# Doubling eight triangular inverses in one chain, with half of them held in the other head's partitions

## The chip, the cores and the metric

The kernel runs on one core of a Trainium2 chip. The metric is the device time of one execution in microseconds. Before the change it is 2000.85 us, the median of 3 runs (1999.77 to 2000.95).

## The reference, cut to what matters

Two transformer blocks run one after the other on 512 tokens of width 1024. The second block has a mixer with two groups of 8 heads: stick-breaking attention, and the RWKV-7 recurrence that is touched here. For each head and each token, with a 64 x 64 state S,

```
S_t = S_{t-1} diag(w_t) + (S_{t-1} a_t) b_t^T + v_t k_t^T ;  y_t = S_t r_t
```

The kernel computes it in 8 chunks of 64 tokens. Inside a chunk the vectors S_{t-1} a_t depend on one another through a strictly triangular 64 x 64 matrix A, so the inverse of a unit triangular matrix, (I - A)^-1, is wanted for each chunk and head: 8 chunks x 8 heads. Everything is in fp32.

## The kernel before

The second block's mixer is `mix2`. Heads are taken two at a time, four times (f = 0 to 3): head one lies in partitions 0 to 63, head two in 64 to 127. For each f, `rw_solve` prepares the chunk matrices and their inverses, and `rw_scan` (of the f before, at the same time) carries the state over the 8 chunks. After them come the stick-breaking heads.

All small products are 64 x 64 x 64 in fp32. `pair` (L400) issues one product for each of the two heads, with rows and output in the same half of the partitions: two opposite corners of the 128 x 128 array. `turn` is a `pair` with the identity, which transposes. In the trace each fp32 product is two MATMUL instructions with a load of weights each, so a pair is four.

The inverse is found by doubling, in `double(q)` (L1905 to L1934), for q = 0 (chunks 0 to 3) and q = 1 (chunks 4 to 7) as two chains of steps that run beside each other. A tile `tmt` holds for four chunks the inverse so far (index 1) and its transpose (index 0). First the transposes are made (4 turns, a ScalarE copy at L1913). Then there are five levels (blocks of 2, 4, 8, 16, 32):

- step one: 4 pairs, A times the transpose, into a PSUM bank, and VectorE masks the level's blocks out of it into z (L1921);
- step two: 4 pairs for the transpose (`tmt`, z; not at the last level) and 4 pairs for the inverse (z, `tmt`) into the two halves of one bank, and VectorE adds both onto `tmt` (L1930; at the last level only the inverse, L1933).

Everything has a tag of PSUM banks: `c` has 3 banks in turn, used by the solve and by the norms and transposes of the stick-breaking queries, keys and values; `pt` has 3, used by the scan.

The order of TensorE's instructions is written at build time by `weave` (L409). It keeps a clock of its own, on which a pair costs 55 ns and half of its two products' time (`pair`, last line), a VectorE or ScalarE operation a fixed part and a part by its size (`after`, with `SEM` and `SEM2` for the way there and back). A stream (`rw_solve`, `rw_scan`, norms) that has to wait yields the time at which it can go on. While no stream is ready, `weave` puts in "fillers": matmuls 128 x 128 x 512 of the projections that the mixer has to make anyway (`sb_steps`, `rw_steps`, through `dense_steps`). It puts in as many as the wait needs at 214 ns each, at least four (`MINF`):

```
self.fill(max(MINF, math.ceil((t - self.clock) / 214)))
```

It also paces them, by `WORK[f]` and the supply of the period. The supply of a period is limited: a queue entry opens only when its period has come and when `heads` and `scans` have got far enough, and where none is open the clock jumps, and the engine really waits. In the trace all matmuls of these helpers have line L339.

Of the kernel before, what the change touches and what calls it, by code (L numbers as in the profile page):

```python
# [9 lines left out]
F32 = mybir.dt.float32  # L10
# [3 lines left out]
AF = mybir.ActivationFunctionType  # L14
OP = mybir.AluOpType
# [278 lines left out]
class K:  # L294
# [106 lines left out]
    def pair(self, o, l, r, start=False, stop=False):  # L401

        t = self.clock
        for hh in (0, 1):
            p = slice(64 * hh, 64 * hh + 64)
            self.mm(o(p), l(p), r(p), start=start, stop=stop)
        self.clock = t + 55 + (self.clock - t) / 2

    def turn(self, o, x):  # L409

        self.pair(o, x, lambda p: self.ident[p, p], True, True)
# [1385 lines left out]
    def rw_solve(self, f, u, ag):  # L1797

        nc, V, S, P, C = self.nc, self.nc.vector, self.nc.scalar, self.nc.gpsimd, self.C2
        yield lambda: (f, 1) in u  # L1800
        xk = u[f, 1]
        t2 = self.rt
# [8 lines left out]
        x = self.after("S", 512, self.after("V", 512))  # L1811
        t, kf, bo = self.tmp("rt"), xk, self.tmp("bo", "rt")
# [4 lines left out]
        for half in (0, 1):  # L1817
            ps = self.bank("c")
            for b2 in (0, 1):
                b = 2 * half + b2  # L1820
# [3 lines left out]
            w = lambda x: x[:, hs].rearrange("p (b t) -> p b t", b=2)  # L1824
# [15 lines left out]
        def tok(n, src):  # L1840
            ps = self.bank("c")
            for c in range(8):
                cs = slice(64 * c, 64 * c + 64)
                self.turn(lambda p: ps[p, cs], lambda p: src[p, cs])
            d = t2(f"tok{n}")
            S.activation(d, ps, AF.Copy)
            self.after("S", 512)
            return d

        yield lambda: (f, 0) in u  # L1850
        r = u[f, 0]
# [6 lines left out]
        vt = tok(2, v)  # L1858
        ar = self.rp.tile([128, 8, 2, 64], F32, name="ar", tag="ar", bufs=2)
# [10 lines left out]
        x = self.after("V", 1024)  # L1870
# [17 lines left out]
        x = self.after("V", 512)  # L1888
# [3 lines left out]
        yield from mat(0, bb)  # L1892
        ab, ak = mats

        bc = lambda x: x.unsqueeze(1).to_broadcast([128, 4, 64])
        tt = []
        for q in (0, 1):
            d = self.rp.tile([128, 2, 4, 64], F32, name=f"tmt{q}", tag=f"tmt{q}", bufs=2)
            V.tensor_tensor(d[:, 1], ab[:, 4 * q:4 * q + 4, 0:64], bc(C["m1t"]), op=OP.mult)
            V.tensor_tensor(d[:, 1], d[:, 1], bc(C["eye"]), op=OP.add)  # L1900
            x = self.after("V", 512)
            tt.append(d)
        self.rws = dict(ar=ar, ab=ab, ak=ak, bt=bt, kt=kt, vt=vt, tt=tt, dec=dec, bon=bon)

        sq4 = lambda ps: ps[:, 0:256].rearrange("p (c t) -> p c t", t=64)  # L1905

        def double(q):

            d = tt[q]
            ps = sq4(self.bank("c"))  # L1910
            for c in range(4):
                self.turn(lambda p: ps[p, c], lambda p: d[p, 1, c])
            S.activation(d[:, 0], ps, AF.Copy)  # L1913
            w = self.after("S", 256)
            for l in range(5):
                yield w
                ps = sq4(self.bank("c"))
                for c in range(4):
                    self.pair(lambda p: ps[p, c], lambda p: ab[p, 4 * q + c, 0:64], lambda p: d[p, 0, c], True, True)
                z = sq4(t2(f"z{q}", 256, 1))  # L1920
                V.tensor_tensor(z, ps, bc(C["lev"][:, 64 * l:64 * l + 64]), op=OP.mult)  # L1921
                yield self.after("V", 256)
                ps = self.bank("c").rearrange("p (i c t) -> p i c t", i=2, t=64)
                if l < 4:
                    for c in range(4):
                        self.pair(lambda p: ps[p, 0, c], lambda p: d[p, 1, c], lambda p: z[p, c], True, True)
                for c in range(4):
                    self.pair(lambda p: ps[p, 1, c], lambda p: z[p, c], lambda p: d[p, 1, c], True, True)
                if l < 4:
                    V.tensor_tensor(d, ps, d, op=OP.add)  # L1930
                    w = self.after("V", 512)
                else:
                    V.tensor_tensor(d[:, 1], ps[:, 1], d[:, 1], op=OP.add)  # L1933
                    w = self.after("V", 256)  # L1934

        yield x
        yield double(0), double(1)

    def rw_scan(self, f, u, o, g2, sg, w):

        nc, V, S, P, C = self.nc, self.nc.vector, self.nc.scalar, self.nc.gpsimd, self.C2
        ar, ab, ak, bt, kt, vt, tt, dec, bon = (w[k] for k in ("ar", "ab", "ak", "bt", "kt", "vt", "tt", "dec", "bon"))
        t2 = self.rt
        st = std = None
        y = o
        for c in range(8):
            cs = slice(64 * c, 64 * c + 64)
            tc = tt[c // 4][:, 1, c % 4]
            b = self.bank("pt")[:, 0:64]
            self.pair(lambda p: b[p], lambda p: ak[p, c, 0:64], lambda p: vt[p, cs], True, st is None)  # L1950
            if st is not None:
                yield w
                self.pair(lambda p: b[p], lambda p: ar[p, c, 0], lambda p: st[p], False, True)
            x = t2("xc", 64)
            S.activation(x, b, AF.Copy)
            w = self.after("S", 64)
            if st is not None and c < 7:
                std = t2("std", 64)
                V.tensor_scalar(std, st, dec[:, c:c + 1], None, op0=OP.mult)
                self.after("V", 64)  # L1960
            yield w
            b1 = self.bank("pt")[:, 0:64]
            self.pair(lambda p: b1[p], lambda p: tc[p], lambda p: x[p], True, True)
            u = t2("uc", 64)
            S.activation(u, b1, AF.Copy)
            w = self.after("S", 64)
            if c < 7:
                b2 = self.bank("pt")[:, 0:64]
                self.pair(lambda p: b2[p], lambda p: kt[p, cs], lambda p: vt[p, cs], True, False)
            yield w  # L1970
            if c < 7:
                self.pair(lambda p: b2[p], lambda p: bt[p, cs], lambda p: u[p], False, True)
                ns = t2("st", 64)
                if st is None:
                    V.tensor_scalar(ns, b2, dec[:, c:c + 1], None, op0=OP.mult)
                else:
                    V.scalar_tensor_tensor(ns, b2, dec[:, c:c + 1], std, op0=OP.mult, op1=OP.add)
                w = self.after("V", 64)
            b3 = self.bank("pt")[:, 0:64]
            self.pair(lambda p: b3[p], lambda p: vt[p, cs], lambda p: ak[p, c, 64:128], True, False)  # L1980
            self.pair(lambda p: b3[p], lambda p: u[p], lambda p: ab[p, c, 64:128], False, st is None)
            if st is not None:
                self.pair(lambda p: b3[p], lambda p: st[p], lambda p: ar[p, c, 1], False, True)
            V.tensor_copy(y[:, cs], b3)
            x = self.after("V", 64)
            if c < 7:
                st = ns

        yield x
        m = self.bank("pt")  # L1990
        self.mm(m, self.blk, y, start=True, stop=True)
        V.scalar_tensor_tensor(y, m, -1.0 / 64, y, op0=OP.mult, op1=OP.add)
        yield lambda: not self.squares
        self.squares = 1
        sq = t2("hsq", 512, 1)
        S.activation(sq, y, AF.Square)
        x = self.after("S", 512, self.after("V", 512))
        ps = self.bank("pt")
        self.mm(ps, g2[:, 128 * f:128 * f + 128], sg, start=True, stop=True)
        V.scalar_tensor_tensor(bon, bon, self.vec("rw_ln_b_2", f), ps, op0=OP.add, op1=OP.mult)  # L2000
        V.scalar_tensor_tensor(y, y, self.vec("rw_ln_w_2", f), ps, op0=OP.mult, op1=OP.mult)
        self.after("V", 1024)
        yield x
        rr = yield from self.root("pt", sq, 1.0 / 64, self.eps[1])
        self.squares = 0
        V.tensor_tensor(y, y, rr, op=OP.mult)
        self.roots -= 1
        yield self.after("V", 512)
        V.tensor_tensor(o, y, bon, op=OP.add)
        yield self.after("V", 512)  # L2010
        self.scans = f + 1
# [40 lines left out]
```

## Time and profile before

| what | value |
|---|---|
| median of 3 runs | 2000.85 us |
| the profiled execution's own time | 2004.94 us |
| its span, first to last instruction | 2003.1 us |
| TensorE matmuls, busy share of the span | 96% |
| TensorE weight loads, busy share | 74% |
| VectorE, ScalarE busy share | 54%, 39% |
| mean granted TensorE clock | 0.978 |
| mixer of the second block, solves and scans | about 1185 to 1515 us of the span |

Times are counted from the span's start. "Busy" is the time in which an instruction of the engine is under way; matmuls overlap one another, so their pace is read from the starts of successive groups in the timeline, not from their durations.

### The profile page before, as it was taken

The page shows a single profiled execution, that of the slowest core. Times are in us where ns is not written, and L with a number is a line of the kernel's source. Part 1 is how long each engine was busy: PE and PEld are TensorE (multiplying, and loading weights), DVE is VectorE, ACT ScalarE, POOL GpSimd, SP SyncE. Part 2 cuts the span into 40 slices and gives each one's busy share as a digit, 9 for nine tenths or more (in the row PEclk, how much of TensorE's full clock was granted, in tenths as well). Part 3 has the DMA queues.
Part 4 walks back from the last instruction along what each step waited for, and adds up shares of the span by engine and source line. Part 5 has one row for each costly group of instructions (what it writes and reads, how often), then busy time and mean ns, then how long its engine had stood idle before and what let it go on. Part 6 is the DMA issues. An engine that isn't in the chain of part 4 may idle for free.

```text
span 2003.1 us, 27567 instructions
## 1 busy us (share of the span) xinstructions
PE 1926.2 (96%) x11492; PEld 1475.2 (74%) x11492; DVE 1079.5 (54%) x1798; ACT 782.2 (39%) x1353; POOL 147.8 (7%) x117
## 2 busy tenths in 40 slices
PE   5889999889999998999999999999999999999999
PEld 2766666668888886888888877677667778888887
DVE  6588875662434346543434555565657674444343
ACT  3666776442323233322222453322335652222221
POOL 3340110130000002000000000000002200000000
PEclk8999999889999998999999999999999899999999
DMA  7124123312322221223232321110101022323222
GB/s 292 56 98 143 65 87 135 106 63 84 105 84 100 90 94 61 98 84 105 85 105 85 105 92 44 43 44 23 38 18 33 1 105 84 106 85 105 87 98 90
DMA packets 27342, 171.54 MB, mean 86 GB/s; under 512 B 3153, under 2 KB 3409, under 8 KB 9041
## 3 DMA queue, kind: packets, MB, share of 16 engines
q1 hardware_dynamic: 23472, 163.44, 23.4%
q10 hardware_dynamic: 3744, 6.34, 0.9%
q8 instruction: 90, 1.47, 0.3%
q14 instruction: 36, 0.29, 0.0%
HBM read 167.67 MB, written 2.10 MB: 85 GB/s over the span
## 4 chain that ended last, share of the span: by engine, by line
PE 80%; ACT 2%; DVE 2%; POOL 1%; issue 1%; DMA 0%; ACTq 0%; POOLq 0%; DVEq 0%
PE ps_mm L339 45%; PE ps_s L339 22%; PE ps_c L339 7%; PE ps_pt L339 4%; PE ps_o L339 1%; POOL xr L1308 0%; PE ps_pt L878 0%; ACT whi L243 0%; POOL x L1357 0%; DMA x<-in_x 0%; DVE wlo L249 0%; PE ps_mm L734 0%; DVE hl L1372 0%; DVE y L1356 0%; POOL hl L1315 0%
## 5 line engine op out<-in xcount | busy, mean ns | idle before, releaser
L243 ACT ACTIVATE whi<-w 128x1024 fp32r<-128x1024 f32 (+4 forms) x277 | 274.7, 994 | 787.0 <-PE ps_mm L339 481.5
L339 PE MATMUL ps_mm<-hh,whi 128*128 128x512 f32 x1304 | 528.7, 406 | 21.7 <-ACT whi L243 9.3
L339 PE MATMUL ps_mm<-hh,wlo 128*128 128x512 f32 x1304 | 528.7, 406 | 6.1 <-DVE wlo L249 6.1
L339 PE MATMUL ps_mm<-hl,whi 128*128 128x512 f32 x1304 | 529.6, 406 | 2.9 <-DVE hl L1315 1.2
L249 DVE TENSOR_TENSOR wlo<-w,whi 128x1024 fp32r<-128x1024 f32 (+7 forms) x316 | 325.2, 1036 | 155.8 <-ACT whi L243 155.4
L339 PEld LDWEIGHTS ps_mm<-hh,whi 128*128 128x128 f32 x1304 | 248.2, 191 | 89.5 <-ACT whi L243 12.6
L339 PEld LDWEIGHTS ps_mm<-hh,wlo 128*128 128x128 f32 x1304 | 248.3, 190 | 74.7 <-DVE wlo L249 9.6
L339 PEld LDWEIGHTS ps_mm<-hl,whi 128*128 128x128 f32 x1304 | 248.1, 190 | 68.2 <-issue 4.5
L339 PE MATMUL ps_s<-vl,whi 128*128 128x512 f32 x352 | 137.2, 390 | 0.0
L339 PE MATMUL ps_s<-vh,wlo 128*128 128x512 f32 x352 | 137.0, 389 | 0.0
L339 PE MATMUL ps_s<-vh,whi 128*128 128x512 f32 x352 | 136.7, 389 | 0.0
L1413 DVE TENSOR_TENSOR su<-ps_mm,rr 128x512 f32<-128x512 f32 x42 | 29.0, 691 | 139.9 <-PE ps_mm L339 139.9
L1425 DVE SCALAR_TENSOR_TENSOR x<-ps_s,x 128x512 f32<-128x512 f32 x48 | 33.2, 692 | 129.4 <-PE ps_s L339 129.4
L339 PE MATMUL ps_s<-uh,whi 128*128 128x512 f32 x256 | 101.1, 395 | 0.0
L339 PE MATMUL ps_s<-ul,whi 128*128 128x512 f32 x256 | 101.1, 395 | 0.0
L339 PE MATMUL ps_s<-uh,wlo 128*128 128x512 f32 x256 | 101.1, 395 | 0.0
L1412 DVE TENSOR_TENSOR sg<-ps_mm,rr 128x512 f32<-128x512 f32 x42 | 29.1, 692 | 103.9 <-PE ps_mm L339 99.6
L339 PEld LDWEIGHTS ps_s<-vl,whi 128*128 128x128 f32 x352 | 66.1, 188 | 14.4 <-DVE vl L759 0.6
L339 PEld LDWEIGHTS ps_s<-vh,wlo 128*128 128x128 f32 x352 | 66.1, 188 | 13.9
L339 PEld LDWEIGHTS ps_s<-vh,whi 128*128 128x128 f32 x352 | 66.1, 188 | 13.8
L339 PEld LDWEIGHTS ps_s<-ul,whi 128*128 128x128 f32 x256 | 48.0, 187 | 11.8
L339 PEld LDWEIGHTS ps_s<-uh,whi 128*128 128x128 f32 x256 | 48.0, 187 | 11.7
(559 smaller groups left out, 2723.1 us busy)
## 6 DMA issues: line engine op xcount, KB each, us to landing
w<-in_gu SPq DMA_DIRECT2D x44, 1024.0 KB, 4.9
w<-in_win SPq DMA_DIRECT2D x17, 1024.0 KB, 5.0
w<-in_wada SPq DMA_DIRECT2D x16, 1024.0 KB, 5.4
w<-in_wup SPq DMA_DIRECT2D x16, 1024.0 KB, 4.8
w<-in_wdn SPq DMA_DIRECT2D x16, 1024.0 KB, 4.8
w<-in_dn SPq DMA_DIRECT2D x16, 1024.0 KB, 4.8
wa<-in_wada SPq DMA_DIRECT2D x8, 1024.0 KB, 13.4
w<-in_dn SPq DMA_DIRECT2D x8, 768.0 KB, 4.4
```

Source lines behind the costliest of these rows:

```text
L243: self.nc.scalar.activation(hi[:, :n], src, AF.Copy)
L249: self.nc.vector.tensor_tensor(lo[:, o:m], src[:, o:m], hi[:, o:m], op=OP.subtract)
L339: self.last_pe = self.nc.tensor.matmul(o, l, r, start=start, stop=stop, skip_group_check=True)
L1412: V.tensor_tensor(g, pg, r, op=OP.mult)
L1413: V.tensor_tensor(v, pu, r, op=OP.mult)
L1425: V.scalar_tensor_tensor(self.x[m], ps, 0.5, self.x[m], op0=OP.mult, op1=OP.add)
```

## The change

`four` issues four products, one in each corner of the array, and puts 55 ns and a quarter of their time on the planner's clock. `other` gives the opposite half of the partitions. The two chains `double(0)` and `double(1)` become one, written out in `rw_solve`. For chunks 4 to 7 (`db`, from `e`) the inverse and z are kept in the opposite half: at the start 4 `four` calls transpose `e` and also copy it across with an identity. In each level, step one is 4 `four` calls (corner pair one into bank `pa`, the crossing pair into bank `pb`) and two masks; step two is 4 `four` calls for the two transposes (not at the last level), then 8 pairs for the inverses, then three VectorE adds where there were two. `rw_scan` swaps partitions for chunks 4 to 7 on the way to the inverse and back.

```
@@ class K
+    def four(self, *g):
+        t = self.clock
+        for o, l, r in g:
+            for hh in (0, 1):
+                p = slice(64 * hh, 64 * hh + 64)
+                self.mm(o(p), l(p), r(p), start=True, stop=True)
+        self.clock = t + 55 + (self.clock - t) / 4
+
+    def other(self, p):
+        return slice(64 - p.start, 128 - p.start)
@@ rw_solve
         bc = lambda x: x.unsqueeze(1).to_broadcast([128, 4, 64])
-        tt = []
-        for q in (0, 1):
-            d = self.rp.tile([128, 2, 4, 64], F32, name=f"tmt{q}", tag=f"tmt{q}", bufs=2)
-            V.tensor_tensor(d[:, 1], ab[:, 4 * q:4 * q + 4, 0:64], bc(C["m1t"]), op=OP.mult)
-            V.tensor_tensor(d[:, 1], d[:, 1], bc(C["eye"]), op=OP.add)
+        sw = self.other
+        tt = [self.rp.tile([128, 2, 4, 64], F32, name=f"tmt{q}", tag=f"tmt{q}", bufs=2) for q in (0, 1)]
+        zz = lambda q: t2(f"z{q}", 256, 1).rearrange("p (c t) -> p c t", t=64)
+        e = zz(1)
+        for q, d in ((0, tt[0][:, 1]), (1, e)):
+            V.tensor_tensor(d, ab[:, 4 * q:4 * q + 4, 0:64], bc(C["m1t"]), op=OP.mult)
+            V.tensor_tensor(d, d, bc(C["eye"]), op=OP.add)
             x = self.after("V", 512)
-            tt.append(d)
...
-        def double(q):
...
-        yield x
-        yield double(0), double(1)
+        eight = lambda: self.bank("c").rearrange("p (i c t) -> p i c t", i=2, t=64)
+        da, db = tt
+        yield x
+        pa, pb = eight(), eight()
+        for c in range(4):
+            self.turn(lambda p: pa[p, 0, c], lambda p: da[p, 1, c])
+        for c in range(4):
+            self.four((lambda p: pa[p, 1, c], lambda p: e[p, c], lambda p: self.ident[p, p]),
+                      (lambda p: pb[sw(p), 0, c], lambda p: self.ident[p, p], lambda p: e[p, c]))
+        S.activation(da[:, 0], pa[:, 0], AF.Copy)
+        S.activation(db[:, 0], pa[:, 1], AF.Copy)
+        w = self.after("S", 512)
+        S.activation(db[:, 1], pb[:, 0], AF.Copy)
+        self.after("S", 256)
+        for l in range(5):
+            yield w
+            pa, pb = eight(), eight()
+            for c in range(4):
+                self.four((lambda p: pa[p, 0, c], lambda p: ab[p, c, 0:64], lambda p: da[p, 0, c]),
+                          (lambda p: pb[sw(p), 0, c], lambda p: ab[p, 4 + c, 0:64], lambda p: db[p, 0, c]))
+            za, zb = zz(0), zz(1)
+            for z, ps in ((za, pa), (zb, pb)):
+                V.tensor_tensor(z, ps[:, 0], bc(C["lev"][:, 64 * l:64 * l + 64]), op=OP.mult)
+                w = self.after("V", 256)
+            yield w
+            pa, pb, pc = eight(), eight() if l < 4 else None, eight()
+            if l < 4:
+                for c in range(4):
+                    self.four((lambda p: pa[p, 0, c], lambda p: da[p, 1, c], lambda p: za[p, c]),
+                              (lambda p: pb[sw(p), 0, c], lambda p: db[p, 1, c], lambda p: zb[p, c]))
+            for c in range(4):
+                self.pair(lambda p: pa[p, 1, c], lambda p: za[p, c], lambda p: da[p, 1, c], True, True)
+            for c in range(4):
+                self.pair(lambda p: pc[p, 0, c], lambda p: zb[p, c], lambda p: db[p, 1, c], True, True)
+            if l < 4:
+                V.tensor_tensor(da, pa, da, op=OP.add)
+                V.tensor_tensor(db[:, 0], pb[:, 0], db[:, 0], op=OP.add)
+                self.after("V", 512)
+            else:
+                V.tensor_tensor(da[:, 1], pa[:, 1], da[:, 1], op=OP.add)
+            w = self.after("V", 256)
+            V.tensor_tensor(db[:, 1], pc[:, 0], db[:, 1], op=OP.add)
+            self.after("V", 256)
@@ rw_scan, for each chunk c
+            at = self.other if c > 3 else lambda p: p
             b = self.bank("pt")[:, 0:64]
-            self.pair(lambda p: b[p], lambda p: ak[p, c, 0:64], lambda p: vt[p, cs], True, st is None)
+            self.pair(lambda p: b[at(p)], lambda p: ak[p, c, 0:64], lambda p: vt[p, cs], True, st is None)
             if st is not None:
                 yield w
-                self.pair(lambda p: b[p], lambda p: ar[p, c, 0], lambda p: st[p], False, True)
+                self.pair(lambda p: b[at(p)], lambda p: ar[p, c, 0], lambda p: st[p], False, True)
...
-            self.pair(lambda p: b1[p], lambda p: tc[p], lambda p: x[p], True, True)
+            self.pair(lambda p: b1[at(p)], lambda p: tc[p], lambda p: x[p], True, True)
```

## Rows read from the trace of the kernel before

**Rows 1.** The page, part 1: engines, busy us (share of span) x instructions.

```profile
PE 1926.2 (96%) x11492; PEld 1475.2 (74%) x11492; DVE 1079.5 (54%) x1798; ACT 782.2 (39%) x1353; POOL 147.8 (7%) x117
```

**Rows 2.** Busy time by stretch: length, PE, PEld, DVE, ACT, POOL, clock, DMA.

```profile
1185.00:1490.00 305.00, 298.14 (x3925) 215.41 (x3925) 180.28 (x354) 101.49 (x210) 0.00 (x0) 0.99 0.11 38
1490.00:1650.00 160.00, 156.44 (x879) 114.05 (x876) 113.58 (x219) 93.32 (x183) 27.42 (x24) 0.95 0.13 44
1407.90:1411.30 3.40, 3.40 (x11) 2.26 (x12) 0.42 (x1) 0.22 (x1) 0.00 (x0) 0.50 0.82 289
```

**Rows 3.** TensorE's waits from 1185 to 1490 us: total us, times, longest.

```profile
PE ps_c L339 <- DVE tmt L1930: 2.6, 3, 1.5
PE ps_c L339 <- DVE z L1921: 2.1, 3, 0.9
```

**Rows 4.** Instructions on `tmt`: count, min/median/max ns, first and last start, forms.

```profile
L339 PE MATMUL ps_c<-tmt,am x640: 218/218/267, 1223.3 to 1480.9; 64*64 64x64 f32 x160
L339 PE MATMUL ps_c<-tmt,z x640: 218/218/267, 1226.0 to 1482.2; 64*64 64x64 f32 x160
L339 PE MATMUL ps_c<-z,tmt x512: 218/218/267, 1225.5 to 1479.0; 64*64 64x64 f32 x171
L339 PE MATMUL ps_c<-ident,tmt x128: 218/218/267, 1221.1 to 1444.4; 64*64 64x64 f32 x128
```

**Rows 5.** Timeline of TensorE: start us, us, engine, line, what, count [idle before].

```profile
1229.35 0.39 PE L339 MATMUL ps_mm<-hh,wlo 128*128 128x512 f32 x1
1229.58 0.39 PE L339 MATMUL ps_mm<-hh,whi 128*128 128x512 f32 x1
1229.90 1.15 PE L339 MATMUL ps_c<-tmt,am 64*64 64x64 f32 x32
1230.98 0.51 PE L339 MATMUL ps_mm<-hl,whi 128*128 128x512 f32 x1
...
1232.11 0.68 PE L339 MATMUL ps_c<-z,tmt 64*64 64x64 f32 x16
...
1317.47 0.68 PE L339 MATMUL ps_c<-tmt,am 64*64 64x64 f32 x16
1318.08 0.50 PE L339 MATMUL ps_mm<-hl,whi 128*128 128x512 f32 x1
```

**Rows 6.** The same view: the first of 60 visits of the doubling to TensorE.

```profile
1221.12 1.15 PE L339 MATMUL ps_c<-ident,tmt 64*64 64x64 f32 x32
```

**Rows 7.** The same view: products 64 x 64 x 128, and products 128 x 64 x 128.

```profile
1209.68 1.96 PE L339 MATMUL ps_c<-ar,ei 64*64 64x128 f32 x32
1211.57 0.50 PE L339 MATMUL ps_mm<-hh,wlo 128*128 128x512 f32 x1
...
1566.11 0.44 PE L339 MATMUL ps_mm<-am,sq 128*64 128x128 f32 x4
...
1566.38 0.39 PE L339 MATMUL ps_mm<-tok,sq 128*64 128x256 f32 x2
```

**Rows 8.** Instructions on `tmt`: weight loads of 64 and of 128 columns.

```profile
L339 PEld LDWEIGHTS ps_c<-tmt,am x640: 129/135/135, 1223.3 to 1480.9; 64*64 64x64 f32 x160
...
L339 PEld LDWEIGHTS ps_c<-u,tmt x8: 183/186/190, 1492.0 to 1558.0; 64*128 64x128 f32 x8
```

**Rows 9.** Instructions on `tmt` and on z: VectorE's adds and masks.

```profile
L1930 DVE TENSOR_TENSOR tmt<-ps_c,tmt x32: 684/692/693, 1226.7 to 1479.7; 128x512 f32<-128x512 f32 x32
...
L1921 DVE TENSOR_TENSOR z<-ps_c,mb x40: 415/425/426, 1224.0 to 1481.2; 128x256 f32<-128x256 f32 x40
```

**Rows 10.** Timeline of TensorE where no filler was open, with what ended its idle time.

```profile
1405.63 0.68 PE L339 MATMUL ps_c<-tmt,am 64*64 64x64 f32 x16 [1.45 <-DVE tmt L1930]
1407.17 0.68 PE L339 MATMUL ps_c<-tmt,z 64*64 64x64 f32 x16 [0.85 <-DVE z L1921]
...
1477.45 1.12 PE L339 MATMUL ps_c<-qx,c 128*128 128x512 f32 x2 [0.63 <-ACT qx L1443]
...
1481.75 0.68 PE L339 MATMUL ps_c<-tmt,z 64*64 64x64 f32 x16 [0.62 <-DVE z L1921]
```

More of the change, by code (lines that the diff above doesn't have):

```diff
@@ L1901, in rw_solve @@
+        e = zz(1)
+        for q, d in ((0, tt[0][:, 1]), (1, e)):
+            V.tensor_tensor(d, ab[:, 4 * q:4 * q + 4, 0:64], bc(C["m1t"]), op=OP.mult)
+            V.tensor_tensor(d, d, bc(C["eye"]), op=OP.add)
             x = self.after("V", 512)
-            tt.append(d)
         self.rws = dict(ar=ar, ab=ab, ak=ak, bt=bt, kt=kt, vt=vt, tt=tt, dec=dec, bon=bon)
-        sq4 = lambda ps: ps[:, 0:256].rearrange("p (c t) -> p c t", t=64)
-        def double(q):
-            d = tt[q]
-            ps = sq4(self.bank("c"))
-            for c in range(4):
[L1912 to L1917, printed above, removed]
-                for c in range(4):
[L1919 to L1934, printed above, removed]
```

## The prediction

> **What bounds the kernel now.** I read the page first: TensorE has work under way in 96% of the span and no other engine comes near [rows 1]. Then the busy time by stretch, for the part that the change touches: from 1185 to 1490 us TensorE is busy 298.14 of 305.00 us, VectorE 180.28, and the clock is at its upper level but for about 1% [rows 2]. The reader is to see that there is hardly any idle time to win. The list of TensorE's waits says the same: those that the doubling causes come to 2.6 and 2.1 us in 305 [rows 3]. So the doubling's latency is already covered by fillers, which have to run anyway. What counts is how much of TensorE's time the doubling itself takes, and whether its waits stay covered.
>
> That time is read from the timeline, start to start. A visit of 32 instructions lasts 1230.98 - 1229.90 = 1.08 us and one of 16 lasts 1318.08 - 1317.47 = 0.61 us [rows 5]. So 16 instructions cost 0.47 us, a pair (four of them) 0.117 us, and every visit has a fixed 0.14 us. Fillers follow one another at 0.23 us, but four of them between two visits take 1.13 us and not 0.92 [rows 5], so going to the fillers and back costs another 0.21. A visit costs 0.35 us besides its products.
>
> What limits a pair? With 128 instead of 64 moving columns the same 32 instructions take 1211.57 - 1209.68 = 1.89 us [rows 7]. That is 0.81 more for 16 turns of the two corners: 0.051 us for 64 columns in one corner, where the whole turn takes 0.47 / 8 = 0.058. So each corner is nearly always streaming, and the other two corners stand empty.
>
> **The change, part by part.**
>
> *Fours for pairs.* The doubling has 640 + 640 + 512 + 128 = 1920 matmul instructions [rows 4], 480 for each f: 240 products, 120 pairs. After it each f has 40 fours (4 at the start, 20 in the first steps, 16 in the second) and 44 pairs: 4 turns, and 8 inverse pairs in each of five levels. 36 fours replace two pairs each. At the start 4 turns and 4 fours stand where 8 turns stood, as the copy across is added there.
>
> What a four costs, the trace does not show. Lower bound: 0.117 us, since each corner still has two instructions to run. Upper bound by the nearest rows: two pairs one after the other, 0.235. Two corners that share their rows do run side by side in this trace: four instructions of 128 rows x 64 columns, two in each half of the columns, take 1566.38 - 1566.11 = 0.27 us [rows 7]. At 2 x 0.051 us each, one after the other would be 0.41. Two corners that share their columns are not shown; the change gives them different banks. I take 0.117, as the nearest row has no sign of a shared path. Gain: 36 x 4 x 0.117 = **16.9 us**; the start is even.
>
> *Fewer visits.* I count 60 visits of the doubling: 14, 16, 14 and 16 for the four f, the first at 1221.12 and the last at 1481.75 [rows 6, 10]. The two chains drift against each other and need three or more a level. The one chain needs one for the start and two a level: 11 for each f, 44 in all. The fillers are the same matmuls, in fewer batches. Gain: 16 x 0.35 = **5.6 us**. Bounds: 2 us if the fillers get split at other waits instead, 5.6 if not.
>
> *VectorE.* Per level, two masks and two adds, 2 x 0.425 + 2 x 0.692 = 2.23 us, become two masks, one large add and two of the masks' size: 0.692 + 4 x 0.425 = 2.39 us [rows 9]. This costs nothing while fillers cover it. By the planner's formula the masks ask for 1168 ns, six fillers, which take 6 x 0.23 + 0.21 = 1.6 us against 0.85 of VectorE. The adds ask for 1442 ns, seven fillers, 1.8 us against 1.1, and part of that lies under the 8 pairs. VectorE's other queue, the fillers' own weight parts, is unchanged; it is busy 59% of the stretch [rows 2]. If the cover is gone, a wait costs 0.6 to 1.5 us [rows 10], about 1.0.
>
> *Is there cover?* The start wants five fillers and the levels 6 and 7: 5 + 4 x 13 + 6 = 63 for each f. Before, 14 visits with four behind each took about 52, and 16 about 63, and two periods still ended bare [rows 10]. With the same supply I leave two waits bare in f = 0, three in f = 2, two in f = 3: 7 x 1.0 = 7.0 us.
>
> *A new wait.* Step two now holds all three `c` banks until VectorE has added. A norm or transpose of the fillers that comes right behind it waits for a bank, with every filler behind it in TensorE's order. Its kind of wait was 0.63 [rows 10]; now it would be the large add and the way there and back, 0.9. I count two: 1.8 us. Together 8.8 instead of 4.7: **4.1 us lost**.
>
> *Edits at nothing.* The scan's crossed pairs are as many as before, in corners as empty as the others. ScalarE's three copies at the start lie under five fillers. There are no DMAs in the change.
>
> Sum: -16.9 - 5.6 + 4.1 = -18.4 us. The profiled execution took 2004.94 us, so 1986.5; the median of the runs is 4.1 below it, so I forecast 2000.85 - 18.4, about **1982 us**. Nothing later gives it back: the rest of the program is bound by TensorE too (156.44 of 160.00 in the next stretch, [rows 2]).
>
> Its own range: the clock stands at 0.95 in the next stretch [rows 2], some 16 us at its lower level that cost 8, and one such piece at 1407.90 follows the bare end of f = 2 [rows 2, 10]. The order of work moves, so pieces can go or come, 5 us either way. With the visits at 2 and the bare waits at twice my count it ends at 1991, with all cover found and some clock won at 1972.
>
> **The rivals.**
>
> *The single chain starves.* Two chains cover each other; one has only fillers. If the supply ends a level and a half earlier in every f, 16 waits are bare at 1.1: 17.6 instead of 4.7, and the clock may fall in each. The gain shrinks to about 9: 1992 us. For it: the two bare ends now. Against: the filler count above is near what was used.
>
> *The change doesn't do what it says: a four costs two pairs*, because corners that share their columns take turns at the output. Then 160 x 0.235 stands against 144 x 0.235 + 16 x 0.117, 1.9 lost; with 5.6 and 4.1 the sum is +0.4: 2001 us. For it: no row shows such corners at work together. Against: nothing in the rows limits the outputs.
>
> *Slower: loads do not lie under matmuls of the same rows.* A load of 64 columns is 0.051 us shorter than one of 128 [rows 8], so it takes some 0.051 as well. If in each half of the rows load and matmul alternate for two corners, a four takes 4 x (0.051 + 0.051) = 0.41 us. Then 160 x 0.41 = 65.6 against 144 x 0.235 + 16 x 0.117 = 35.7, with 5.6 and 4.1: +28, 2029 us. It makes the kernel slower by over 4 us from a four of 0.26 us on. Against it: today a corner turns every 0.058 us with 0.051 of streaming, so its own next load does lie under its matmul [rows 5, 7].
>
> The Trainium skill's page "TensorE: Matmul & The Clock Gate" (Part 3: Packing small matmuls — row/col tiling, "The mechanism") states such a rule: weight loads overlap matmuls in flight only where they target other rows. Taken at its word it gives the last rival's 2029 us where the rows give 1982. This trace does not agree with it for one corner, where the load of the same rows leaves 0.007 us uncovered.
>
> **How the numbers follow.** The forecast has 0.76, the starved chain 0.08, a four at two pairs 0.10, the alternating loads 0.06. A measurement of this kernel can tell about 0.2%, 4 us, from no change. Faster is the first two, 0.84; same the third, 0.10; slower the last, 0.06. The forecast's own range, 1972 to 1991, holds most of its 0.76; going on to 1994 takes in the starved chain, 0.80 in all. The other two are left out.
>
> **What would show it.** A first step's visit, still 32 instructions, lasts 0.61 us instead of 1.08, and a second step's, 64 instructions, about 1.55. If a first step still takes 1.08, the corners take turns; over 1.5, the loads alternate. The doubling has about 44 visits. TensorE's waits for `tmt` and z, and of norms for a `c` bank, come to about 9 us; if they are near 18, the chain starves. The pieces at the lower clock level should sum to what they do now. The forecast fails by its sizes if the windows of the solves shrink by much less than 4 us each with the visits as short as said.

## The result and the profile after

The kernel after takes 1974.63 us (median of 4 runs, 1968.61 to 1978.25), the kernel before 2000.87 (median of 4) beside it: 26.2 us less, ratio 0.9867 (95% interval 0.9853 to 0.9882). I had forecast 1982.0, between 1972 and 1994. A second set of runs of the same kernel gave 1976.09 us (ratio 0.9881, 0.9869 to 0.9894).

The profiled execution is the fastest of the runs, 1968.61 us, with a span of 1966.8 us and a granted clock of 0.983. Part 1 of its page:

```profile
PE 1890.1 (96%) x11556; PEld 1446.8 (74%) x11556; DVE 1077.4 (55%) x1814; ACT 781.3 (40%) x1357; POOL 149.5 (8%) x117
```

TensorE still has work under way in 96% of the span [rows 1]; its busy time has fallen by 36 us, the span by 36 us, part of it clock as told below, and the other engines do what they did. The bound is the same one, with less in it. The busy time by stretch (length, PE, PEld, DVE, ACT, POOL, clock, DMA), as [rows 2]:

```profile
1185.00:1490.00 305.00, 301.18 (x4270) 214.98 (x4269) 199.34 (x415) 117.43 (x248) 3.64 (x3) 1.00 0.11 38
1490.00:1650.00 160.00, 155.48 (x744) 117.04 (x743) 108.77 (x193) 87.60 (x159) 25.59 (x21) 0.99 0.18 63
```

The same 305 us now hold 345 more matmuls, because the last solve's last products start at 1447.4 and not at 1482.2 us [rows 4]. All of TensorE's waits for the doubling in the solves (1185 to 1480 us: total, times, longest) come to one:

```profile
PE ps_c L339 <- DVE z L1940: 0.4, 1, 0.4
```

Before they were 2.6 and 2.1 us [rows 3]. And the timeline of TensorE (start, us, what, count, idle before) through one and a half levels of the doubling in f = 0:

```profile
1222.09 0.69 PE L339 MATMUL ps_c<-tmt,am 64*64 64x64 f32 x32
1222.71 0.50 PE L339 MATMUL ps_mm<-hl,whi 128*128 128x512 f32 x1
...
1224.77 0.69 PE L339 MATMUL ps_c<-z,tmt 64*64 64x64 f32 x32
1225.28 1.10 PE L339 MATMUL ps_c<-tmt,z 64*64 64x64 f32 x32
1226.31 0.50 PE L339 MATMUL ps_mm<-hh,whi 128*128 128x512 f32 x1
...
1233.64 0.50 PE L339 MATMUL ps_mm<-hh,wlo 128*128 128x512 f32 x1
1233.98 0.39 PE L339 MATMUL ps_mm<-hh,whi 128*128 128x512 f32 x1
1234.21 0.40 PE L339 MATMUL ps_mm<-hl,whi 128*128 128x512 f32 x1
1234.44 0.40 PE L339 MATMUL ps_mm<-hh,wlo 128*128 128x512 f32 x1
1235.20 0.95 PE L339 MATMUL ps_c<-z,tmt 64*64 64x64 f32 x30 [0.35 <-DVE z L1940]
```

A first step of 32 instructions takes 1222.71 - 1222.09 = 0.62 us where 32 took 1.08 [rows 5], a second step of 64 takes 1226.31 - 1224.77 = 1.54. There are 44 visits. Between visits there are often only four fillers, and behind the four from 1233.64 on 0.35 us was short; that is the one wait of the list.

**Where the time came from.** I added up the starts of TensorE's matmuls, each instruction's time being the distance to the next start, from the solves' first transposes to the first product into `ps_s` (1202.6 to 1643.0 us before). A wait thus counts with the instruction before it. For an equal clock I take the second profile of the kernel after (1976.06 us; 20.5 us of this region at the lower clock level, as in the profile of before):

| us of TensorE | doubling | scan | other solve products | the rest | sum |
|---|---|---|---|---|---|
| before | 71.6 | 43.0 | 27.7 | 298.2 | 440.5 |
| after, second profile | 46.4 | 40.4 | 27.4 | 298.4 | 412.6 |
| after, first profile | 46.4 | 40.4 | 27.4 | 291.2 | 405.4 |

So 25.2 of the 27.9 us come from the doubling itself and 2.6 from the scan, which I had put at nothing. The rest is the same at an equal clock, to 0.2 us. The last row shows 7.2 us that are not the kernel's: the two profiles of one program differ by a long piece of lower clock and a short one. For the long one, busy time in the same stretch, the second profile first, then the first (length, PE, PEld, DVE, ACT, POOL, clock, DMA):

```profile
1509.20:1522.85 13.65, 13.65 (x46) 8.16 (x44) 6.17 (x13) 6.03 (x13) 4.91 (x5) 0.50 0.13 52
```

```profile
1509.20:1522.85 13.65, 12.92 (x72) 8.97 (x71) 10.91 (x23) 11.09 (x23) 7.03 (x6) 1.00 0.05 20
```

TensorE is busy without a gap in the first, at half the clock, and gets 46 matmuls through instead of 72. Because such a piece comes and goes, the table of the experiments has a last column beside the medians: span times mean granted clock, averaged over the runs, an estimate of the time that the work would take at the full clock level. The clock is given to three digits, so one run's figure is good to about 1 us. It is of use only near the usual clock: a run of the kernel before took 2003.34 us with 0.933 listed, and a slow run of early_adds, which stands in no figure below, 2107.04 us with 0.837.

### The profile page after: what moved, and what is told of

Same layout as the page of the kernel before. It is cut to its first block, busy times and chain, and to the rows that moved or that the text cites. A ratio compares the mean times of both kernels' runs of the same rounds, so it can differ in the third digit from the quotient of the medians.

```text
span 1966.8 us, 27713 instructions
## 1 busy us (share of the span) xinstructions
PE 1890.1 (96%) x11556; PEld 1446.8 (74%) x11556; DVE 1077.4 (55%) x1814; ACT 781.3 (40%) x1357; POOL 149.5 (8%) x117
## 4 chain that ended last, share of the span: by engine, by line
PE 79%; DVE 3%; ACT 2%; issue 1%; POOL 1%; DMA 0%; POOLq 0%; ACTq 0%; DVEq 0%
PE ps_mm L339 44%; PE ps_s L339 23%; PE ps_c L339 6%; PE ps_pt L339 4%; PE ps_o L339 1%; PE ps_pt L890 1%; POOL xr L1320 0%; DVE wlo L249 0%; ACT whi L243 0%; POOL x L1369 0%; DMA x<-in_x 0%; PE ps_mm L746 0%; DVE hl L1384 0%; DVE y L1368 0%; POOL hl L1327 0%
## 5 line engine op out<-in xcount | busy, mean ns | idle before, releaser
L249 DVE TENSOR_TENSOR wlo<-w,whi 128x1024 fp32r<-128x1024 f32 (+7 forms) x316 | 321.8, 1026 | 158.3 <-ACT whi L243 157.9
L1361 DVE TENSOR_TENSOR y<-y,ps_s 128x512 f32<-128x512 f32 x24 | 16.5, 687 | 74.0 <-PE ps_s L339 74.0
L339 PEld LDWEIGHTS ps_s<-uh,wlo 128*128 128x128 f32 x256 | 48.0, 187 | 11.8
```

Of the source, the lines that this page charges most:

```text
L249: self.nc.vector.tensor_tensor(lo[:, o:m], src[:, o:m], hi[:, o:m], op=OP.subtract)
L339: self.last_pe = self.nc.tensor.matmul(o, l, r, start=start, stop=stop, skip_group_check=True)
L1361: V.tensor_tensor(y[m], y[m], ps, op=OP.add)
```

## The experiments

Each expectation says what its theories are. C is the account that I held when it was written, K the part of it about the clock, and the other letters are rivals. "Doubling" is always the sum of its starts, as in the table above.

| kernel | median us (runs) | ratio to before, 95% | at full clock |
|---|---|---|---|
| before_again (unchanged) | 2000.85 (12) | 0.9999, 0.9986 to 1.0011 | 1960.9 |
| after | 1974.63 (4) | 0.9867, 0.9853 to 0.9882 | 1932.8 |
| after_again (unchanged) | 1976.09 (4) | 0.9881, 0.9869 to 0.9894 | 1932.1 |
| one_chain_pairs | 1989.60 (5) | 0.9945, 0.9933 to 0.9957 | 1951.2 |
| corners_apart | 1981.81 (6) | 0.9907, 0.9892 to 0.9923 | 1939.6 |
| all_corners | 1970.35 (4) | 0.9847, 0.9834 to 0.9860 | 1934.2 |
| ask_less | 1976.24 (5) | 0.9881, 0.9861 to 0.9900 | 1933.8 |
| ask_more | 1977.35 (5) | 0.9883, 0.9863 to 0.9902 | 1939.3 |
| all_corners_less | 1966.35 (4) | 0.9829, 0.9809 to 0.9848 | 1929.5 |
| early_adds | 1970.84 (4) | 0.9846, 0.9830 to 0.9861 | 1932.6 |
| early_corners | 1966.25 (5) | 0.9825, 0.9806 to 0.9845 | 1930.4 |

**One chain without the corners** (one_chain_pairs). One chain as in the kernel after, but all chunks in their own partitions, and pairs throughout:

```
-                self.four((lambda p: pa[p, 0, c], lambda p: ab[p, c, 0:64], lambda p: da[p, 0, c]),
-                          (lambda p: pb[sw(p), 0, c], lambda p: ab[p, 4 + c, 0:64], lambda p: db[p, 0, c]))
+                self.pair(lambda p: pa[p, 0, c], lambda p: ab[p, c, 0:64], lambda p: da[p, 0, c], True, True)
+            for c in range(4):
+                self.pair(lambda p: pb[p, 0, c], lambda p: ab[p, 4 + c, 0:64], lambda p: db[p, 0, c], True, True)
...
-            at = self.other if c > 3 else lambda p: p
+            at = lambda p: p
```

> One chain with two steps a level, but everything in its own partitions and in pairs, at the pair's price on the planner's clock; no copy across, no crossing in the scan. Theory C: only the visits (60 to 44, 5.6 us) and the bare waits (some 4 us) are won, about 1991 us. Theory M: nearly the whole gain is here, about 1975 to 1980 us.

Measured 1989.60 us, and the timeline of TensorE has the old pace again:

```profile
1221.93 1.15 PE L339 MATMUL ps_c<-tmt,am 64*64 64x64 f32 x32
1223.01 0.51 PE L339 MATMUL ps_mm<-hl,whi 128*128 128x512 f32 x1
...
1225.07 1.15 PE L339 MATMUL ps_c<-z,tmt 64*64 64x64 f32 x32
1226.05 1.10 PE L339 MATMUL ps_c<-tmt,z 64*64 64x64 f32 x32
1227.08 0.50 PE L339 MATMUL ps_mm<-hh,whi 128*128 128x512 f32 x1
```

1.08 us for 32 instructions and 2.01 for 64. By the sum of the starts the doubling takes 63.2 us, so the single chain alone saves 8.4 of 71.6, and the corners 16.8 more. Its list of waits has none for `tmt` or z. So the chain on its own, which my prediction had losing cover, loses none: 4.4 of the 8.4 us are waits of before that are gone (of its 4.7, 0.4 stand behind a filler and so not in the doubling), and the 4.0 that are left I put down to the visits, 43 for 60; no run parts them further.

**The corners one after the other** (corners_apart). The same fours, issued as four pairs for one pair of corners and then four for the other. On the planner's clock they count as before:

```
+    def fours(self, *g):
+        jobs = [(o, l, r, c) for o, l, r in g for c in range(4)]
+        for k in range(0, 8, 2):
+            t = self.clock
+            for o, l, r, c in jobs[k:k + 2]:
+                for hh in (0, 1):
+                    p = slice(64 * hh, 64 * hh + 64)
+                    self.mm(o(p, c), l(p, c), r(p, c), start=True, stop=True)
+            self.clock = t + 55 + (self.clock - t) / 4
```

> The same products and the same price on the planner's clock, but each group of four fours is issued as four pairs in one pair of corners and then four pairs in the other, so that the corners take turns. Theory C (the gain is four corners at work at once): a first step's visit of 32 instructions goes from 0.62 to about 1.08 us, a second step's from 1.54 to about 2.0, ten groups for each f at 0.47 us each: 18.8 us slower than the changed kernel, about 1993. Theory M (the gain is one chain in place of two, fewer visits and shorter waits): the visits keep their number, and the time stays within 4 us of the changed kernel, 1971 to 1979, because the queue of TensorE finds the free corners by itself.

Measured 1981.81 us. The timeline at the start of f = 0, where all products of weights z (`ident,z`) are issued before all those with z moving (`z,ident`), and the first step behind it:

```profile
1220.68 0.46 PE L339 MATMUL ps_c<-ident,z 64*64 64x64 f32 x10
1220.93 0.27 PE L339 MATMUL ps_c<-z,ident 64*64 64x64 f32 x2
1220.97 0.28 PE L339 MATMUL ps_c<-ident,z 64*64 64x64 f32 x3
...
1222.65 0.98 PE L339 MATMUL ps_c<-tmt,am 64*64 64x64 f32 x32
1223.55 0.50 PE L339 MATMUL ps_mm<-hl,whi 128*128 128x512 f32 x1
```

`z,ident` starts at 1220.93, ahead of `ident,z` that come before it in the program (in the mixer, `ordered` puts each TensorE instruction behind the one before). By the recorded starts, a matmul whose corner is free overtakes those that wait for theirs, so part of the gain stays without the interleaving, and neither theory holds as written: a first step takes 0.90 us, between the 0.62 of the kernel after and the 1.08 that I expected here. The doubling takes 54.3 us, 7.9 more and not the 18.8 more that the old pace would have brought: of the 16.8 that the corners bring, 8.9 come by themselves and 7.9 only with the order corner by corner.

**The inverses' products as fours too** (all_corners). The zb, `tmt` products write across, and are added back in two operations of 64 partitions:

```
-                self.pair(lambda p: pa[p, 1, c], lambda p: za[p, c], lambda p: da[p, 1, c], True, True)
-            for c in range(4):
-                self.pair(lambda p: pc[p, 0, c], lambda p: zb[p, c], lambda p: db[p, 1, c], True, True)
+                self.four((lambda p: pa[p, 1, c], lambda p: za[p, c], lambda p: da[p, 1, c]),
+                          (lambda p: pc[sw(p), 0, c], lambda p: zb[p, c], lambda p: db[p, 1, c]))
...
-            V.tensor_tensor(db[:, 1], pc[:, 0], db[:, 1], op=OP.add)
+            for p in (slice(0, 64), slice(64, 128)):
+                V.tensor_tensor(db[p, 1], pc[sw(p), 0], db[p, 1], op=OP.add)
```

> The 8 pairs for the inverses become 4 fours too: the product for chunks 4 to 7 goes across into the other half, and VectorE brings it back with two adds of 64 partitions each in place of one of 128. Theory C: a second step's visit goes from 1.54 to about 1.08 us and the last one's from 1.08 to 0.61, 5 x 0.47 for each f: 9.3 us, about 1965 us. Rival: the added 0.42 us of VectorE in every level makes the masks late, waits for z appear in the list of TensorE's waits, and less than 3 us are won, 1972 or more.

Measured 1970.35 us, with a second step of 1.09 us. But at full clock it is 1.7 us above the kernel after, not below, and within the spread of its runs: its median is lower because three of its four runs had a clock of 0.983 where those of the kernel after had 0.976 to 0.983. The doubling took 43.6 us, 2.8 less, where 9.3 less were expected. Most of what is missing is in its waits (1185 to 1480 us: total, times, longest):

```profile
PE ps_c L339 <- DVE tmt L1952: 4.2, 5, 1.2
PE ps_c L339 <- DVE z L1940: 2.8, 3, 1.2
...
PE ps_c L339 <- DVE tmt L1953: 0.7, 1, 0.7
...
PE ps_c L339 <- DVE tmt L1959: 0.7, 1, 0.7
```

8.4 us in all, 4.2 of them in the 43.6 and 4.2 behind a filler; some 2 us of the missing stay open. Only 2.8 us are for the masks, which the rival named; 5.6 are for the adds. That the shorter visits no longer cover the adds is argued, not shown, and it is not all: in VectorE's timeline operations of other streams run between the visit and the release in seven of the nine waits of the doubling's own products.

**The same program twice** (after_again, before_again).

> The changed kernel once more, to see how far its times spread. Its four runs went from 1968.6 to 1978.3 us, where the kernel before stayed within 1.2 us. If the clock is what spreads them (theory K), the pieces of the span at the lower clock level differ from profile to profile by several us, and the median stays between 1970 and 1978. If the order of work is what spreads them, the clock pieces agree and stretches outside them differ.

> The kernel before, unchanged, for a second profile of the same program. The kernel after has been profiled twice with the same order of instructions: 1968.6 us, with one 3.4 us piece at the lower clock level behind 1490 us, and 1976.1 us, with a 13.65 us piece besides. Theory K (the pieces of lower clock come and go by themselves, the changed order of work does not set them): the long piece at 1575 us in the profile of the kernel before comes, goes or moves as well; without it the profiled execution is 6 to 7 us shorter, 1998 us. Rival P (the order of the work sets the pieces, so the changed kernel has won some clock): pieces of 3.41, 3.41, 13.65 and 3.36 us at the same starts within a microsecond, 2005 us again.

In after_again the doubling (46.4 us), the scan and the other solve products agree with the first profile to 0.02 us, while the pieces of lower clock in the region are 20.5 us for 3.4: theory K. In before_again the piece of 13.65 us at 1575 us is not there; in that stretch the granted clock is 0.92 instead of 0.50 (before first, then before_again):

```profile
1575.15:1588.80 13.65, 13.65 (x50) 9.96 (x51) 9.68 (x19) 7.55 (x16) 3.78 (x4) 0.50 0.00 1
```

```profile
1575.15:1588.80 13.65, 13.65 (x75) 10.20 (x76) 9.30 (x18) 10.31 (x20) 6.79 (x6) 0.92 0.00 1
```

Its profiled execution took 1998.98 us, 6.0 less. The long piece comes and goes in both kernels, so it is no part of the change, and theory K holds for it. The short piece of 3.41 us behind the bare end of f = 2 comes in both profiles of before, at 1407.90 [rows 2] and at 1406.5; the kernel after has none in the mixer before 1490 us. Nor has ask_more, though three of its periods end bare, so whether a bare end brings such a piece stays open.

**How much cover the waits want** (ask_less, ask_more). Both waits of a level ask the planner for 400 ns less, or for 800 ns more:

```
-            yield w
+            yield w - 400
...
-            yield w
+            yield w - 400
```

> The changed kernel, where the doubling's two waits in each level ask the planner for 400 ns less (four or five fillers instead of six or seven). Theory C (four fillers, 1.12 us, are enough for what the waits really need, at most 1.1 us by the gaps that were seen bare): TensorE's waits for the masks and the adds stay under 2 us in all, the doubling takes 46.4 us as before within 1.5, and the time is the changed kernel's, 1968 to 1977 by the clock piece. Rival S (the planner's six and seven were needed, as my prediction took them): most of 40 waits are short by some 0.4 us; waits of 10 us or more, and 1980 us or more.

> The changed kernel, where the doubling's two waits in each level ask for 800 ns more (ten or eleven fillers). Theory C, with a supply that ends: a solve's ten waits ask for some 105 fillers, where about 50 stand in its doubling now; so five or six of ten are left without any in each of the four solves, though some have a step of the scan. 12 to 24 bare waits at 0.9 us each, 11 to 22 us: 1980 to 1998 us. Rival A (the supply never ends where the doubling stands, or the planner spreads what is left, so asking changes nothing): waits under 3 us and 1968 to 1977 us.

Asked for less, the waits are 2.6 us in all and the doubling takes 49.2 us; the time is unchanged (1976.24 us, 1933.8 at full clock). It is a little more than theory C allowed (2 us, 47.9) and far from rival S. Asked for more, the waits of TensorE are

```profile
PE ps_c L339 <- DVE z L1940: 5.9, 7, 1.2
PE ps_c L339 <- DVE tmt L1953: 3.8, 3, 1.3
```

and the timeline shows where: behind the last fillers of a period, as here in f = 1.

```profile
1320.57 0.39 PE L339 MATMUL ps_mm<-hh,wlo 128*128 128x512 f32 x1
1320.89 0.69 PE L339 MATMUL ps_c<-tmt,am 64*64 64x64 f32 x32
1322.47 0.95 PE L339 MATMUL ps_c<-z,tmt 64*64 64x64 f32 x30 [0.89 <-DVE z L1940]
...
1325.60 0.69 PE L339 MATMUL ps_c<-tmt,am 64*64 64x64 f32 x32 [1.28 <-DVE tmt L1953]
```

So the supply does end, as my prediction said, if each wait takes ten fillers: 10 waits, 9.7 us, somewhat under the 12 to 24 that theory C asked for. The kernel costs 6.8 us more at full clock, not the whole of the doubling's 11.6 more (58.0 us); that fits fillers that go out in fewer batches, as "the rest" takes 284.4 us at full clock, where the second profile of the kernel after has 288.2. That is the loss I had forecast for the kernel after; it is there only when the planner is asked for too much.

**Two versions meant to beat both kernels.** all_corners_less is all_corners with 400 ns less asked. early_adds adds the two transposes under the pairs of the inverses, which get a bank of their own; early_corners does the same with all products as fours, the crossing ones into a bank of the scan's:

```
+                for d, ps in ((da, pa), (db, pb)):
+                    V.tensor_tensor(d[:, 0], ps[:, 0], d[:, 0], op=OP.add)
+                    w = self.after("V", 256)
             for c in range(4):
-                self.pair(lambda p: pa[p, 1, c], lambda p: za[p, c], lambda p: da[p, 1, c], True, True)
+                self.pair(lambda p: pc[p, 0, c], lambda p: za[p, c], lambda p: da[p, 1, c], True, True)
             for c in range(4):
-                self.pair(lambda p: pc[p, 0, c], lambda p: zb[p, c], lambda p: db[p, 1, c], True, True)
+                self.pair(lambda p: pc[p, 1, c], lambda p: zb[p, c], lambda p: db[p, 1, c], True, True)
...
-                V.tensor_tensor(da, pa, da, op=OP.add)
-                V.tensor_tensor(db[:, 0], pb[:, 0], db[:, 0], op=OP.add)
...
@@ early_corners, instead of the pairs
+            pd = self.bank("pt").rearrange("p (i c t) -> p i c t", i=2, t=64)
...
+                self.four((lambda p: pc[p, 0, c], lambda p: za[p, c], lambda p: da[p, 1, c]),
+                          (lambda p: pd[sw(p), 0, c], lambda p: zb[p, c], lambda p: db[p, 1, c]))
```

> The kernel all_corners (the inverses' products as four corners too), again with 400 ns less asked by each wait. There TensorE waited 8.4 us for the masks and adds, at the ends of the periods. Theory C: those waits are there because the shorter steps leave more of the work to fillers that the first waits have used up; with four or five in place of six or seven the supply reaches the end, the waits fall to 3 us or less, the doubling from 43.6 to 38 to 40 us, and the time from 1970.4 to 1964 to 1967 us (without a long clock piece). Rival L (the two adds of 64 partitions make the real need longer than four fillers): waits of 8 us or more stay, and move from the ends into the middles of the periods; 1970 us or more.

> The changed kernel, where the two transposes of step two are added first, under the eight pairs of the inverses (these get a bank of their own), so that the next step one needs only adds that are done by then. The planner puts two fillers there instead of four to six; the number of visits stays 44. Theory C (the waits of the changed kernel are covered already and only TensorE's own time counts): nothing to win, doubling 46.4 us within 1.5, full-clock work within 2 us of the changed kernel, 1970 to 1978 us. Rival M (going to the fillers and back is what is left, and fillers freed from these waits go out in longer batches): 2 to 5 us less. Rival V (VectorE, with four small operations instead of three in a level, gets the masks out later): waits for z of 4 us or more, and slower by as much.

> The same early adds, with the inverses' products as four corners too (as in all_corners; the crossing half goes to a bank of the scan's). all_corners_less kept 9.5 us of waits, seven of them for the last add, since its visit of 1.09 us leaves less time for four VectorE adds. Theory C: here the next step one waits for two adds that lie under the second fours, so the waits for tmt fall from 5.8 to under 2 us, the doubling to 34 to 37 us against 39.6, and the time is at or under that of all_corners_less, 1960 to 1966 us. Rival V: VectorE now has two masks and five adds in a level, 3 us, which the fillers of a level (ten, 2.3 us, and the visits' 1.7) barely cover; the masks come late instead: waits for z of 6 us or more, 1966 to 1972 us.

early_adds changes nothing at full clock (1932.6 us; doubling 47.5, waits for `tmt` 1.0 us): there was nothing left to cover, as theory C had it. all_corners_less is the fastest at full clock, 1929.5 us, and 1966.35 at the median, but not by theory C. The doubling is down to 39.6 us as expected, but its waits did not fall to 3 us: 9.5 us of them stay, and they have moved into the middles of the periods, as rival L said. There they stand behind fillers, and so 7.8 us of them count with the rest. The timeline of TensorE, then of VectorE:

```profile
1234.49 0.65 PE L339 MATMUL ps_c<-tmt,z 64*64 64x64 f32 x32
1235.07 0.50 PE L339 MATMUL ps_mm<-hh,wlo 128*128 128x512 f32 x1
1235.40 0.39 PE L339 MATMUL ps_mm<-hh,whi 128*128 128x512 f32 x1
1235.63 0.40 PE L339 MATMUL ps_mm<-hl,whi 128*128 128x512 f32 x1
1235.87 0.40 PE L339 MATMUL ps_mm<-hh,wlo 128*128 128x512 f32 x1
1237.21 0.69 PE L339 MATMUL ps_c<-tmt,am 64*64 64x64 f32 x32 [0.94 <-DVE tmt L1952]
```

```profile
1235.09 0.48 DVE L1825 TENSOR_SCALAR rt<-orw,vecs 128x512 f32<-128x512 f32 x1
1235.48 0.42 DVE L1953 TENSOR_TENSOR tmt<-ps_c,tmt 128x256 f32<-128x256 f32 x1
1235.82 0.74 DVE L1667 SCALAR_TENSOR_TENSOR u<-ud,vecs,u 128x511 f32<-128x511 f32 x1
1236.47 0.69 DVE L1952 TENSOR_TENSOR tmt<-ps_c,tmt 128x512 f32<-128x512 f32 x1
1237.19 0.86 DVE L1959 TENSOR_TENSOR tmt<-ps_c,tmt 64x256 f32<-64x256 f32 x2
```

From 1235.07 on the wait needs 2.1 us, but not for the reason that rival L gave. The two adds of 64 partitions (L1959) start only at the release. Ahead of it VectorE does two adds of the doubling, 0.42 and 0.69 us, and two operations of other streams, 0.48 us before the first and 0.74 us between them. In all seven waits of the doubling for an add it is the large one (L1952) that releases TensorE, with L1959 behind it and other streams' work ahead of it. With the second fours of early_corners behind the two adds that matter, the waits for `tmt` fall from 7.1 us (one of them by a norm) to 4.9, not under 2, and those for z rise to 2.6; its doubling takes 45.4 us, not 34 to 37, with more of the waits inside it, and the result, 1966.25 us and 1930.4 at full clock, is no different. Both beat the kernel after by some 9 us at the median, of which 2 to 3 are work by the full-clock figures and the rest is clock. Why their runs, and those of all_corners, have a higher clock than those of the kernel after (0.982 and 0.983 in 12 of 13) stays open; no run here tells it apart.

## Why the prediction was right, and which of its steps was not

**What bounds the kernel** held: TensorE's own time, 96% busy before and after, and every microsecond less of matmuls in the solves is one less at the end.

**Fours for pairs**, 16.9 us: measured 16.8, as the difference of the doubling between one_chain_pairs and the kernel after. A four costs what a pair costs, 0.058 us for each of its two turns. Both rivals that spoke against it have fallen. That a four costs two pairs wanted 1.08 us for a first step, and that loads and matmuls alternate wanted over 1.5; it is 0.62. The rule of the Trainium skill that stood behind the last one ("TensorE: Matmul & The Clock Gate", Part 3: Packing small matmuls — row/col tiling, "The mechanism") does not agree with this trace: every four has two corners on each half of the rows, each with loads of its own, and runs at the pace of a pair.

**Fewer visits**, 5.6 us: 60 became 44, as counted. In the doubling some 4.0 us go with them, 0.24 for each of the 17 that one_chain_pairs saves; the rest of my 0.35, the way to the fillers and back, would lie in the products around the visits, and those take as much as before (the rest in the table, 298.2 and 298.4 us).

**"Is there cover?" with "A new wait"** is the step that failed: it had 4.1 us lost, by 8.8 us of bare waits. Measured: 0.4 us of waits, so 4.3 won. I counted 63 fillers wanted for each f by the planner's formula, six or seven for a wait, against a supply of 52 to 63, and left the difference bare. In the timeline of after 47, 64, 40 and 55 fillers (up to 8 of them products of other streams) stand between the visits of f = 0 to 3, mostly fewer than I supposed (before 51, 63, 44 and 64 did), and all but nothing is bare. For what a wait needs is shorter than what is asked: bare ones last 0.6 to 1.3 us (ask_more), and four fillers take 1.1. Even the one wait that is left, 0.35 us at 1235.20, is not the masks' own time alone: VectorE is busy with two weight parts of the fillers (L249) for 1.29 us from 1233.52 on, and the masks come behind them. The last visits of f = 0, 2 and 3 have just four fillers before them, the planner's least number (two before the very last), and that is enough. ask_less, which asks for four or five, pays 2.2 us of waits and no time at the end. The mechanism itself is real, as ask_more shows (9.7 us bare at the ends of the periods); the demand was wrong. The waits of norms for a bank that I had put at two did not come at all. The starved chain was the same error, made larger.

**Edits at nothing**: the scan's crossed pairs. I put them at nothing because they are as many as before and their corners as empty. The scan takes 2.6 us less, since they can run beside a pair that is not crossed. In the timeline of after, the chunks 0 to 3 first, then 4 to 7:

```profile
1264.56 0.33 PE L339 MATMUL ps_pt<-xc,tmt 64*64 64x64 f32 x4
1264.72 0.28 PE L339 MATMUL ps_pt<-tok,tok 64*64 64x64 f32 x4
1264.94 0.50 PE L339 MATMUL ps_mm<-hh,wlo 128*128 128x512 f32 x1
...
1268.54 0.27 PE L339 MATMUL ps_pt<-xc,tmt 64*64 64x64 f32 x2
1268.55 0.28 PE L339 MATMUL ps_pt<-tok,tok 64*64 64x64 f32 x2
1268.65 0.23 PE L339 MATMUL ps_pt<-xc,tmt 64*64 64x64 f32 x2
1268.66 0.22 PE L339 MATMUL ps_pt<-tok,tok 64*64 64x64 f32 x2
1268.81 0.51 PE L339 MATMUL ps_mm<-hh,wlo 128*128 128x512 f32 x1
```

Eight instructions take 0.38 us where both pairs want the same corners, and 0.27 where one is crossed. one_chain_pairs, without the crossing, has 44.9 us of scan. Less the idle time behind its own products the scan takes 41.1 us before, 41.5 in one_chain_pairs and 37.9 after.

**The sum.** Measured at an equal clock: -16.8 for the corners, -4.0 for the visits, -4.4 for the waits of before that stood in the doubling, -2.6 for the scan, and -0.3 and +0.2 for the other products of the solve and the rest: -27.9 us in the region. The profiled executions differ by 2004.94 - 1976.06 = 28.9, and the full-clock figures by 1960.9 - 1932.5 = 28.4. My -18.4 has the cover wrong by 8.5 (+4.1 for -4.4), lacks the 2.6 of the scan, and has 1.6 too much for the visits. So the main term came as worked out, but the time came 7.4 us under my 1982, near the end of my range where all cover is found. The medians differ by only 26.2 because of the clock: a mean of 0.980 in the first runs of the kernel after, 0.981 in those of before_again. **The clock** was in my own range as 5 us either way; one long piece is worth 6 to 7 us.

## What to carry to other kernels

Four independent 64 x 64 fp32 products, one in each corner of the array and issued in turn, cost what two cost; where only diagonal products exist, hold half of the data in the opposite partitions, and cross single pairs too where they have a neighbour on the diagonal. Before you subtract lost cover, measure in the timeline what a wait needs and not what the planner asks for it. When the visits become shorter still (all_corners), most of the gain turns into waits for VectorE; look there for other streams' operations ahead of the adds and between them.

## What the runs showed that I had not expected

- Matmuls overtake one another. In corners_apart, and in the scan, products whose corner is free start ahead of those that stand before them in the program; in corners_apart 8.9 of the 16.8 us stay.
- The same program runs for 1968.6 or 1976.1 us by one piece of 13.65 us at the lower level of TensorE's clock (and a short one), in a stretch where TensorE is busy all the time (13.65 of 13.65 us). In the kernel before it comes and goes as well. TensorE had been busy for 5.99 of the 6.83 us ahead of it in the kernel after, but for 6.85 of 6.85 in the kernel before, so idle time ahead of it is not what the two have in common.
- VectorE's order decides waits that look like want of fillers: other streams' operations stand ahead of the masks in the one wait of the kernel after, and ahead of the large add in all seven of all_corners_less.
- Bare waits are not a plain sum: 11.6 us more of doubling in ask_more make 6.8 us more at full clock.
